# Attention: VectorE makes all low parts of the probabilities, where GpSimd made every second one

## The chip, the core and the metric

The kernel runs on one core of a Trainium2 chip. The metric is the device time of one execution in microseconds (us); lower is better. A core has five engines with a queue of instructions each, which run at the same time and wait for one another by semaphores: TensorE (PE in the rows; its weight loads are PEld), VectorE (DVE), ScalarE (ACT), GpSimd (POOL) and SyncE (SP), which here only issues DMAs. Every engine works off its own queue in order, so an instruction that waits holds up all that stands behind it.

## The reference

The program is a backbone of two layers over 1024 latent tokens with 1024 channels and a context of 256 tokens. The first layer has gated linear attention beside a latent attention (MLA), the second a Fourier mixing beside a spatial gate. The change touches only the latent attention:

```python
MLA_HEADS = 8
MLA_SCALE = (MLA_NOPE + MLA_ROPE) ** -0.5          # 64 + 32

def mla_attend(q_nope, q_rope, k_nope, k_rope, v):
    s = (jnp.einsum('bqhd,bkhd->bhqk', q_nope, k_nope, preferred_element_type=jnp.float32)
         + jnp.einsum('bqhr,bkr->bhqk', q_rope, k_rope, preferred_element_type=jnp.float32)) * MLA_SCALE
    p = jax.nn.softmax(s, axis=-1).astype(v.dtype)
    return jnp.einsum('bhqk,bkhd->bqhd', p, v)
...
    o_ml = mla_latent_blocks(qn_l, qr_l,
                             jnp.concatenate([kn_c, kn_l], 1),
                             jnp.concatenate([krot_c, krot_l], 1),
                             jnp.concatenate([vm_c, vm_l], 1))
    y_mla = o_ml * jax.nn.silu(mg_l)
```

There are 1024 queries and 1280 keys (latent tokens and context) for each of eight heads.

## The kernel before

All products are made with fp32r operands in two parts: a high part (the value rounded to fp32r, by ScalarE, line L136) and a low part (the value less its high part, a subtraction of two tiles, line L141). Three matmuls then stand for one: high by high, high by low, low by high (`mm3`, L146 to L148). `split` makes the two parts; its argument `lo_eng` says which engine makes the low part, VectorE if none is given.

The attention works head by head (0 to 7), in `mla`. For a head, `attend` goes over two halves of 512 queries and ten blocks of 128 keys, 20 steps. A step makes a block of scores in a PSUM bank, keys by queries (three matmuls, L1073 to L1075, tile `pss`), ScalarE takes their exponential into SBUF (L118, tile `pexp`), ScalarE makes the high part (L136) and one engine the low part (L141), both into a tile `ph`. Up to five steps later (`LAG`) `second` multiplies the values with them, into a bank `psav`: value high by probability high (L1057), value low by probability high (L1058), value high by probability low (L1059). Only L1059 needs the low part. At the end of a half ScalarE makes the reciprocal of the sums, and VectorE two products, L1066 (two SBUF inputs) and L1067 (one from PSUM).

The engine of a low part is chosen here, where `n` counts the steps of a head:

```python
            k.split(p, None, hi=ph[:, 0, :], lo=ph[:, 1, :], lo_eng=nc.gpsimd if LO_ENG[n % len(LO_ENG)] else None)
...
PREP, LAG, MAXT, EARLY = 1.4, 5, 1.1, 2
LO_ENG = (0, 1)
```

While a head runs, the next one is prepared (`mla_prep`): DMAs from SyncE's queue put its keys and queries in place (L181), then TensorE makes score blocks for the row maxima, for each of eight groups of 128 queries a trio of products over 512, 512 and 256 keys (L998, tile `psm`), and VectorE reduces each of them (L999, tile `mx`). VectorE then takes the maximum of the trios (L1002, tile `m`), TensorE transposes it (L1005), VectorE copies it (L1007) and a DMA from GpSimd's queue puts it into the queries as their 97th row. In heads 6 and 7 GpSimd also multiplies rows of the output weights with a gate (`out_weight`, L1140, tile `owr`), of which ScalarE and VectorE make high and low parts.

A weighted round robin (`weave`) merges these streams, and a scheduler then fixes each engine's order at build time. All score and value products share eight PSUM banks, and the SBUF tiles come from shared pools, so an engine that reads a tile late also gives its buffer back late.

Of the kernel before, what the change touches and what calls it, by code (L numbers as in the profile page):

```python
# [1011 lines left out]
def mla(k):  # L1012
# [28 lines left out]
    def attend(hd):  # L1041
# [27 lines left out]
        for n, (s, j) in enumerate(steps):  # L1069
# [8 lines left out]
            ph = k.b4(F32R, (P, 2, 512), name="ph")  # L1078
            k.split(p, None, hi=ph[:, 0, :], lo=ph[:, 1, :], lo_eng=nc.gpsimd if LO_ENG[n % len(LO_ENG)] else None)
            pp[s, j] = (ph[:, 0, :], ph[:, 1, :])  # L1080
# [29 lines left out]


PREP, LAG, MAXT, EARLY = 1.4, 5, 1.1, 2
LO_ENG = (0, 1)


def even_pre(k):
# [500 lines left out]
```

## Time and profile before

| | |
|---|---|
| median of 3 timed runs | 1145.99 us (1145.76 to 1149.88) |
| the profiled execution | 1150.75 us, span 1149.0 us |
| TensorE busy over the span | 1093.9 us, 95% |
| VectorE busy | 748.1 us, 65% |
| ScalarE busy | 562.2 us, 49% |
| GpSimd busy | 260.2 us, 23% |
| mean granted TensorE clock | 0.981 |

The span goes from the first instruction to the last; the execution's own time holds about 2 us more. Times in rows are counted from the span's start. "Idle before" in a row names what ended the engine's wait. Matmuls are pipelined: one of 512 columns shows some 0.40 us, and the next starts about 0.23 us after it. Several short instructions of one kind in a row stand as one row with their count (x5). The granted clock is 1.00 at TensorE's full 2.4 GHz.

### The profile page before, as it was taken

What the parts mean: (1) busy time and instruction counts of PE and PEld (TensorE: products, weight loads), DVE (VectorE), ACT (ScalarE), POOL (GpSimd) and SP (SyncE); (2) the same over time, 40 slices, a digit from 0 to 9 for tenths busy, and PEclk for the clock granted to TensorE, in tenths of its full rate; (3) what the DMA queues carried; (4) which work ended last, traced back from release to release, by engine and by line L of the source; (5) the groups of instructions that cost most, each with busy time, mean ns of one, the idle gap of its engine ahead of it and who ended that gap; (6) DMA issues with size and microseconds to landing.
All of it is one profiled execution on the core that took longest, in us unless ns stands there. A gap on an engine that the chain in (4) does not pass through costs nothing.

```text
span 1149.0 us, 14557 instructions
## 1 busy us (share of the span) xinstructions
PE 1093.9 (95%) x5288; PEld 867.0 (75%) x5288; DVE 748.1 (65%) x1264; ACT 562.2 (49%) x965; POOL 260.2 (23%) x260
## 2 busy tenths in 40 slices
PE   5889999899999999999999999999999999999997
PEld 3668778788677877767677666888788888888885
DVE  6867694866755685776777677798536633664544
ACT  6285655576563367857777768313422223332000
POOL 3520000000000023423324356443101000122111
PEclk8989999999999999999999999999999999999999
DMA  9635563333535752113302424323400311125111
GB/s 369 246 125 192 206 225 101 133 124 106 194 98 197 217 168 51 34 37 88 70 2 49 124 73 126 132 111 121 143 30 1 110 37 55 56 67 207 56 55 55
DMA packets 41753, 131.89 MB, mean 115 GB/s; under 512 B 5674, under 2 KB 7466, under 8 KB 41683
## 3 DMA queue, kind: packets, MB, share of 16 engines
q1 hardware_dynamic: 35578, 114.77, 31.0%
q0 software_dynamic: 3312, 10.26, 2.3%
q10 hardware_dynamic: 2792, 5.94, 1.3%
q8 instruction: 41, 0.67, 0.2%
q14 instruction: 30, 0.24, 0.1%
HBM read 98.37 MB, written 20.36 MB: 103 GB/s over the span
## 4 chain that ended last, share of the span: by engine, by line
PE 72%; DVE 11%; ACT 6%; issue 4%; POOL 3%; DMA 3%; SPq 0%; POOLq 0%; DVEq 0%; ACTq 0%
PE ps L146 11%; PE ps L148 10%; PE ps L147 10%; PE pso L146 4%; PE pso L148 4%; PE pso L147 4%; PE psm L998 3%; PE pss L1073 3%; PE pss L1074 2%; PE pss L1075 2%; PE psav L1059 2%; PE psav L1057 2%; PE psav L1058 2%; DVE acc L810 1%; DMA qh<-qrh 1%
## 5 line engine op out<-in xcount | busy, mean ns | idle before, releaser
L141 POOL TENSOR_TENSOR ph<-pexp,ph 128x512 fp32r<-128x512 f32 x80 | 108.0, 1354 | 171.5 <-ACT ph L136 143.3
L118 ACT ACTIVATE pexp<-pss 128x512 f32<-128x512 f32 x160 | 93.2, 595 | 64.6 <-PE pss L1075 63.0
L999 DVE TENSOR_REDUCE mx<-psm 128x1 f32<-128x512 f32 (+1 forms) x192 | 102.2, 592 | 13.4 <-PE psm L998 13.0
L146 PE MATMUL ps<-h,hi 128*128 128x512 f32 x256 | 104.0, 418 | 5.4 <-ACT h L331 2.3
L148 PE MATMUL ps<-h,lo 128*128 128x512 f32 x256 | 103.8, 406 | 3.6 <-DVE lo L308 1.7
L141 DVE TENSOR_TENSOR ph<-pexp,ph 128x512 fp32r<-128x512 f32 x80 | 76.2, 957 | 44.3 <-ACT ph L136 42.6
L147 PE MATMUL ps<-h,hi 128*128 128x512 f32 x256 | 102.7, 401 | 0.8 <-DVE h L332 0.8
L146 PE MATMUL pso<-hi,yh 128*128 128x512 f32 x256 | 99.8, 390 | 0.0
L147 PE MATMUL pso<-lo,yh 128*128 128x512 f32 x256 | 99.7, 390 | 0.0
L148 PE MATMUL pso<-hi,yl 128*128 128x512 f32 x256 | 99.0, 389 | 0.0
L136 ACT CAST ph<-pexp 128x512 fp32r<-128x512 f32 x160 | 95.2, 620 | 2.8
L141 DVE TENSOR_TENSOR lo<-wraw,hi 128x1024 fp32r<-128x1024 f32 x37 | 47.0, 1283 | 74.7 <-ACT hi L136 69.7
L146 PE MATMUL ps<-h1h,hi 128*128 128x512 f32 x192 | 75.1, 391 | 0.0
L148 PE MATMUL ps<-h1h,lo 128*128 128x512 f32 x192 | 74.7, 389 | 0.0
L147 PE MATMUL ps<-h1l,hi 128*128 128x512 f32 x192 | 74.7, 389 | 0.0
L1140 POOL TENSOR_TENSOR owr<-owr,rowB 128x1024 f32<-128x1024 f32 x16 | 43.6, 2733 | 118.4 <-DMA owr<-wo 118.4
L1059 PE MATMUL psav<-ph,V 128*96 128x512 f32 x160 | 64.0, 400 | 2.1 <-POOL ph L141 1.1
L1057 PE MATMUL psav<-ph,V 128*96 128x512 f32 x160 | 63.4, 396 | 0.2
L146 PEld LDWEIGHTS ps<-h,hi 128*128 128x128 f32 x256 | 49.0, 193 | 18.3 <-ACT h L331 3.8
L148 PEld LDWEIGHTS ps<-h,lo 128*128 128x128 f32 x256 | 49.2, 192 | 17.5 <-DVE lo L308 2.9
L147 PEld LDWEIGHTS ps<-h,hi 128*128 128x128 f32 x256 | 49.6, 194 | 10.9 <-DVE h L332 1.4
L148 PEld LDWEIGHTS pso<-hi,yl 128*128 128x128 f32 x256 | 48.1, 188 | 10.1
(364 smaller groups left out, 2612.6 us busy)
## 6 DMA issues: line engine op xcount, KB each, us to landing
aw<-ada SPq DMA_DIRECT2D x32, 512.0 KB, 7.5
araw<-ada SPq DMA_DIRECT2D x32, 512.0 KB, 4.8
wraw<-we SPq DMA_DIRECT2D x16, 512.0 KB, 7.5
owr<-wo SPq DMA_DIRECT2D x16, 512.0 KB, 3.5
xr<-x SPq DMA_DIRECT2D x16, 512.0 KB, 6.8
wraw<-wd SPq DMA_DIRECT2D x12, 512.0 KB, 3.5
xt<-x SPq DMA_DIRECT2D x8, 512.0 KB, 6.4
kt<-kn SPq DMA_DIRECT2D x16, 256.0 KB, 3.6
```

What stands on the lines that cost most here:

```text
L118: r = self.nc.scalar.activation(out=out, in_=in_, func=func, **kw)
L136: self.nc.scalar.copy(out=hi, in_=src)
L141: (lo_eng or self.nc.vector).tensor_tensor(out=lo, in0=src, in1=f32(hi), op=ALU.subtract)
L146: t.matmul(out, lhs[0], rhs[0], start=start, stop=False)
L147: t.matmul(out, lhs[0], rhs[1], start=False, stop=False)
L148: return t.matmul(out, lhs[1], rhs[0], start=False, stop=stop)
L998: T.matmul(ps[:, :n], q[0][0:96, i * P:(i + 1) * P], cols(kt[0], s, n)[0:96], start=True, stop=True)
L999: nc.vector.reduce_max(out=mx[:, i, b:b + 1], in_=ps[:, :n], axis=AX.X)
L1057: T.matmul(a[0:96, :], vhi(j, hd), hi, start=j == 0, stop=False)
L1059: T.matmul(a[0:96, :], vhi(j, hd), lo, start=False, stop=j == NK - 1)
L1073: T.matmul(ps, kc[0], q[0][:, o], start=True, stop=False)
L1140: k.nc.gpsimd.tensor_tensor(out=raw, in0=raw, in1=k.ogate, op=ALU.mult)
```

## The change

One tuple is cut to its first entry, so that `LO_ENG[n % len(LO_ENG)]` is 0 for every step and `lo_eng` is never GpSimd in the attention.

```diff
 PREP, LAG, MAXT, EARLY = 1.4, 5, 1.1, 2
-LO_ENG = (0, 1)
+LO_ENG = (0,)
```

The scheduler puts the instructions in another order from there on. On GpSimd's queue, over the whole attention, with `ph` the parts of the probabilities, `qh<-mr` the maxima's DMAs and `owr` the output weights, the difference begins so:

```order
 L1022 MEMSET V 128x8x32 x9
-L141 TENSOR_TENSOR ph<-pexp,ph 128x512 x6
+L181 DMA qh<-mr 1x8x128 x6
+L1140 TENSOR_TENSOR owr<-owr,rowB 128x1024 x2
 L181 DMA qh<-mr 1x8x128
-L141 TENSOR_TENSOR ph<-pexp,ph 128x512 x11
```

All 80 low parts leave the queue; the seven DMAs and the eight `owr` products remain.

On VectorE's queue in head 1, from the first maxima for head 2 to their end (`ph<-pexp,ph` is a low part, `mx<-psm` a maximum, `rl` and `mg` the end of a half), this stood before:

```order
L999 TENSOR_REDUCE mx<-psm 128x1 x2
L1066 TENSOR_TENSOR rl<-rl,mg 64x512
L999 TENSOR_REDUCE mx<-psm 128x1
L1067 TENSOR_TENSOR mg<-psav,rl 64x512
L999 TENSOR_REDUCE mx<-psm 128x1
L141 TENSOR_TENSOR ph<-pexp,ph 128x512
L999 TENSOR_REDUCE mx<-psm 128x1 x3
L141 TENSOR_TENSOR ph<-pexp,ph 128x512
L999 TENSOR_REDUCE mx<-psm 128x1 x6
L141 TENSOR_TENSOR ph<-pexp,ph 128x512
L999 TENSOR_REDUCE mx<-psm 128x1 x6
L141 TENSOR_TENSOR ph<-pexp,ph 128x512
```

and there stands now:

```order
L1067 TENSOR_TENSOR mg<-psav,rl 64x512
L141 TENSOR_TENSOR ph<-pexp,ph 128x512
L999 TENSOR_REDUCE mx<-psm 128x1 x3
L141 TENSOR_TENSOR ph<-pexp,ph 128x512
L999 TENSOR_REDUCE mx<-psm 128x1 x3
L141 TENSOR_TENSOR ph<-pexp,ph 128x512 x2
L999 TENSOR_REDUCE mx<-psm 128x1 x3
L141 TENSOR_TENSOR ph<-pexp,ph 128x512
L999 TENSOR_REDUCE mx<-psm 128x1 x3
L141 TENSOR_TENSOR ph<-pexp,ph 128x512
L999 TENSOR_REDUCE mx<-psm 128x1 x3
L141 TENSOR_TENSOR ph<-pexp,ph 128x512
```

Where six maxima followed each other, a low part now stands behind every trio.

On VectorE's queue in head 6, behind the first 13 maxima, with the low part of an output weight (`lo<-owr,hi`), this stood before:

```order
L141 TENSOR_TENSOR lo<-owr,hi 128x1024
L999 TENSOR_REDUCE mx<-psm 128x1
L141 TENSOR_TENSOR ph<-pexp,ph 128x512 x2
L999 TENSOR_REDUCE mx<-psm 128x1
L141 TENSOR_TENSOR ph<-pexp,ph 128x512
L999 TENSOR_REDUCE mx<-psm 128x1
L141 TENSOR_TENSOR ph<-pexp,ph 128x512
L999 TENSOR_REDUCE mx<-psm 128x1 x2
L141 TENSOR_TENSOR ph<-pexp,ph 128x512
L999 TENSOR_REDUCE mx<-psm 128x1 x6
```

and there stands now:

```order
L141 TENSOR_TENSOR lo<-owr,hi 128x1024
L141 TENSOR_TENSOR ph<-pexp,ph 128x512 x8
L999 TENSOR_REDUCE mx<-psm 128x1 x2
L141 TENSOR_TENSOR ph<-pexp,ph 128x512
L999 TENSOR_REDUCE mx<-psm 128x1 x3
L141 TENSOR_TENSOR ph<-pexp,ph 128x512
L999 TENSOR_REDUCE mx<-psm 128x1 x3
L141 TENSOR_TENSOR lo<-owr,hi 128x1024
L141 TENSOR_TENSOR ph<-pexp,ph 128x512
L999 TENSOR_REDUCE mx<-psm 128x1 x3
```

Twelve low parts and two of weights stand between the first maximum and the last in place of five and one.

## Rows read from the trace of the kernel before

**Rows 1.** Windows: the attention; span, busy us and count of each engine, clock, DMA.

```profile
416.00:718.00 302.00, 291.12 (x1241) 211.00 (x1240) 216.02 (x333) 224.39 (x398) 123.31 (x92) 0.99 0.25 64
```

**Rows 2.** Waits of TensorE in 416 to 718: total us, times, longest.

```profile
PE psm L998 <- DVE mx L999: 2.1, 2, 1.2
PE pss L1073 <- DVE mx L999: 2.0, 2, 1.3
PE psm L998 <- DMA ql<-qrl: 1.7, 1, 1.7
```

**Rows 3.** Groups by form, VectorE in 416 to 718: busy us, mean ns, idle before.

```profile
L141 DVE TENSOR_TENSOR ph<-pexp,ph 128x512 fp32r<-128x512 f32 x80 | 76.2, 957 | 44.3 <-ACT ph L136 42.6 <-issue 0.9 <-POOL ph L141 0.4
```

**Rows 4.** Timeline of VectorE in heads 1 and 2: start us, duration us, instruction, [idle before].

```profile
459.27 2.82 DVE L999 TENSOR_REDUCE mx<-psm 128x1 f32<-128x512 f32 x5
462.06 0.69 DVE L141 TENSOR_TENSOR ph<-pexp,ph 128x512 fp32r<-128x512 f32 x1
462.67 1.01 DVE L999 TENSOR_REDUCE mx<-psm 128x1 f32<-128x256 f32 x2
463.81 0.68 DVE L1066 TENSOR_TENSOR rl<-rl,mg 64x512 f32<-64x512 f32 x1
...
477.06 0.17 DVE L1002 TENSOR_REDUCE m<-mx 128x8 f32<-128x24 f32 x1
...
503.39 4.67 DVE L999 TENSOR_REDUCE mx<-psm 128x1 f32<-128x512 f32 x9
507.97 0.68 DVE L141 TENSOR_TENSOR ph<-pexp,ph 128x512 fp32r<-128x512 f32 x1
```

**Rows 5.** Timeline of TensorE: the transposes of the maxima in heads 0 to 3.

```profile
437.65 0.27 PE L1005 MATMUL psmt<-ident,m 128*8 128x128 f32 x1
...
478.43 0.27 PE L1005 MATMUL psmt<-ident,m 128*8 128x128 f32 x1
...
511.88 0.27 PE L1005 MATMUL psmt<-ident,m 128*8 128x128 f32 x1 [0.17 <-DVE m L1002]
...
560.13 0.27 PE L1005 MATMUL psmt<-ident,m 128*8 128x128 f32 x1
```

**Rows 6.** Timeline of VectorE: ends of the maxima stretches of heads 0, 2, 3, 6.

```profile
420.43 0.69 DVE L999 TENSOR_REDUCE mx<-psm 128x1 f32<-128x512 f32 x1
...
436.81 0.17 DVE L1002 TENSOR_REDUCE m<-mx 128x8 f32<-128x24 f32 x1
...
493.08 3.75 DVE L999 TENSOR_REDUCE mx<-psm 128x1 f32<-128x512 f32 x7 [0.91 <-PE psm L998]
...
511.66 0.17 DVE L1002 TENSOR_REDUCE m<-mx 128x8 f32<-128x24 f32 x1
...
542.44 2.21 DVE L999 TENSOR_REDUCE mx<-psm 128x1 f32<-128x512 f32 x4
...
559.90 0.17 DVE L1002 TENSOR_REDUCE m<-mx 128x8 f32<-128x24 f32 x1
...
645.66 3.93 DVE L999 TENSOR_REDUCE mx<-psm 128x1 f32<-128x512 f32 x7 [3.80 <-PE psm L998]
...
671.47 0.18 DVE L1002 TENSOR_REDUCE m<-mx 128x8 f32<-128x24 f32 x1
671.66 1.23 DVE L141 TENSOR_TENSOR lo<-owr,hi 128x1024 fp32r<-128x1024 f32 x1
```

**Rows 7.** Timeline of GpSimd and VectorE in heads 6 and 7: products of output weights.

```profile
649.47 2.38 POOL L1140 TENSOR_TENSOR owr<-owr,rowB 128x1024 f32<-128x1024 f32 x1 [8.16 <-DMA owr<-wo]
649.88 2.52 DVE L1066 TENSOR_TENSOR rl<-rl,mg 64x512 f32<-64x512 f32 x1 [0.28 <-ACT rl L118]
...
716.43 11.81 POOL L1140 TENSOR_TENSOR owr<-owr,rowB 128x1024 f32<-128x1024 f32 x4
```

**Rows 8.** Waits of TensorE's weight loads in 672 to 718.

```profile
PEld psav L1059 <- POOL ph L141: 4.7, 7, 1.1
```

**Rows 9.** Windows of 2 us in head 4: the granted clock is the last number but two.

```profile
574.00:576.00 2.00, 2.00 (x6) 1.51 (x6) 1.68 (x4) 1.16 (x3) 1.27 (x1) 0.50 0.00 0
```

## The prediction

> **What bounds the kernel now.** I read the windows first, because the change touches one stage only. In the attention (416 to 718 us) TensorE is busy 291 of 302 us [rows 1]; VectorE 216, GpSimd 123. So TensorE's own work sets the length of this stage, and 10.9 us is all that waits can still give back there, with a few us of low clock. Who ends TensorE's waits is in the chain of waits [rows 2]: the row maxima of VectorE, the DMAs that move the next head's queries, and, small, GpSimd's low parts. The groups by form [rows 3] show VectorE's 80 low parts with a mean of 957 ns, well above the 690 of one that is left alone [rows 4].
>
> VectorE is not the bound on average, but it is in places. In seven of the eight heads TensorE also makes the score blocks for the next head's maxima: eight trios `psm` (512, 512 and 256 columns), each followed on VectorE by three reductions L999. I call this the maxima stretch. It ends with L1002 on VectorE, and TensorE's transpose L1005 waits for that, in its queue, with the next products behind it. In head 1 (the second) VectorE works from 459.27 us and reaches L1002 at 477.06 [rows 4]; the transpose starts at 478.43 [rows 5], so VectorE has 1.15 us to spare (L1005 came 0.22 us behind L1002 in head 2, 511.66 to 511.88 [rows 5, 6]). In heads 2 and 3 it has nothing to spare [rows 5, 6].
>
> **The change, part by part.** Every second low part moves from GpSimd's queue to VectorE's, 80 instructions. Prices are those of an undisturbed VectorE [rows 4]: a low part takes 0.61 us of the queue (462.06 to 462.67), a normalizing product L1066 or L1067 is taken as much (its row reads 0.68 where the low part's reads 0.69), a trio of maxima 1.53 (nine instructions, 503.39 to 507.97, are three trios).
>
> Off VectorE goes what GpSimd cost it. 80 low parts at 957 ns in place of 690 are 21 us. On goes 80 x 0.61 = 48.8 us. The net is about +28 us on 216, that is 244 of 302 us: no overload on average, and outside the maxima stretches a low part per 1.4 us of TensorE work (six products at 291.12/1241 = 0.235 us [rows 1]) leaves room. So outside them the move costs nothing: what covers it is VectorE's idle time.
>
> Inside them it counts. By the order of instructions a stretch held 5, 5, 4, 5, 4, 5 and 5 low parts (heads 0 to 6) and now holds 7, 10, 7, 8, 7, 10 and 12. The stretch on VectorE is then: start, eight trios (12.24), low parts at 0.605, two normalizing products where they lie inside (1.21), and waits for ScalarE. Of those waits I know the present ones, as the rest of the stretch, and keep half, since a longer queue hides a part of them; none and all are the two bounds.
>
> Head 1: 12.24 + 5 x 0.605 + 1.21 = 16.48 of 17.79 us now, so 1.31 of waits. After: 459.27 + 12.24 + 6.05 + 1.21 + 0.65 = 479.42, transpose at 479.64 against 478.43: +1.2 us (bounds +0.6 and +1.9). Head 5 has the same order, +1.2.
> Head 2: 15.87 of 18.58 now (493.08 to 511.66 [rows 6]), 2.71 of waits. After: 493.08 + 12.24 + 4.24 + 1.21 + 1.35 = 512.12, transpose 512.34 against 511.88: +0.5 (0 to +1.8). Head 4 has the same seven low parts, but its stretch is long now for low clock (below): +0.1 (0 to +1.8).
> Head 0: three low parts stand ahead of the first maximum, where there was one, so it starts at 420.43 + 2 x 0.605 = 421.64. Then 12.24 + 7 x 0.605 = 438.1; with 0.5 of waits (half of the present 436.81 - 420.43 - 15.27 = 1.1) the transpose is at 438.8 against 437.65: +1.1 (+0.6 to +1.7).
> Head 3: 15.27 of 17.46 now [rows 6], 2.19 of waits. After: 542.44 + 12.24 + 4.84 + 1.1 = 560.62, transpose 560.84 against 560.13: +0.7 (0 to +1.8).
> Together +4.8 us (about +1.8 to +10.9).
>
> Head 6 is the one where GpSimd hurts now. There it also scales output weights (`owr`), and VectorE's operations with two SBUF inputs stand still meanwhile: L1066 takes 2.52 us at 649.88, while GpSimd's `owr` runs from 649.47 for 2.38 [rows 7]. VectorE needs 25.81 us for the stretch [rows 6], of which the undisturbed work is 12.24 + 5 x 0.605 + 1.21 + 1.23 (the low part of an `owr`, 671.66) = 17.7. After: 12.24 + 12 x 0.605 + 1.21 + 2.46 = 23.2. The collisions with low parts on GpSimd are gone, but two `owr` operations remain, and each can hold VectorE for 0 to 2.4 us; with the 1.84 seen in both places (2.52 less 0.68) it is 26.9: +1.0 (-2.6 to +2.2).
> Head 7 has no maxima. There TensorE waits 4.7 us at weight loads for GpSimd's low parts [rows 8], seven times; a load stands about one product, 0.235 us, ahead of its own, so about 4.7 - 7 x 0.235 = 3 reach the products. They go. But GpSimd, now idle, starts the last four `owr` as soon as they land and no longer at 716.43 [rows 7], in the midst of the last low parts; I take half of the gain back: -1.5 (-3 to +2).
> The moved POOL queue also sends the seven small DMAs `qh<-mr` earlier; no wait for one is seen now, so nothing is taken for it. TensorE has as many products as before between a head's last score block and the next maxima, so the waits for query DMAs [rows 2] stay.
>
> Clock: behind a wait for a query DMA (1.7 us [rows 2]) the granted clock fell to 0.50 in 574 to 576 [rows 9], from the 2.4 to the 1.2 GHz level: 1.0 us lost in that slice, taken as 1.5 with its flanks. One or two more such dips are possible with longer waits; the sum holds none.
>
> Sum: +4.8 + 1.0 - 1.5 = +4.3 us on a span of 1149.0 and an own time of 1150.75. That execution lies 4.8 us above the median of the three timed runs, 1145.99, to which I add the difference: 1150.3 us, +0.4%.
>
> The Trainium skill (Perfetto Trace Analysis, Optimizing Scalar/DVE Operations) says that offloading from a saturated VectorE even to GpSimd may make sense, and adds that the two share an SBUF read port, so that it might not help. The first half speaks against this change, and it is rival A below; the second half speaks for it, and rival B is what it would give.
>
> **Rivals.** About 0.5% (5.7 us) is what a measurement here can tell from no change.
> A, slower: VectorE becomes the bound of every maxima stretch. Place: L1002 and the banks that TensorE gets back from L999. The 28 more low parts inside the seven stretches cost 28 x 0.605 = 16.9 us, of which the present waits in VectorE's queue hide part; with all waits kept heads 0 to 5 give +10.9, with heads 6 and 7 as summed +10.4, with one clock dip +11.9: 1158. It decides from the point at which more than half of the waits remain. For it: heads 2 and 3 have no slack now. Against it: the waits are for ScalarE, and a queue that is late no longer waits.
> B, faster: the low parts never delay TensorE, and the collisions vanish. Then TensorE gets back about 3 in head 7 and most of the VectorE waits, 4.1 [rows 2], with one dip, 1.5: -8.6, 1137. For it: the 21 us of inflated low parts; against it: the counts above, and the `owr` collision, which starts the large wait of head 6, stays. The Trainium skill (SBUF — State Buffer, Who interferes with whom) has the mechanism: a VectorE operation with two SBUF inputs and a GpSimd one that reads SBUF exclude each other for a whole instruction; the 2.52 us row agrees.
> C, nothing: the delay at the transpose is made up, since VectorE and ScalarE catch up before TensorE runs dry, and head 7's gain pays for the rest: -1 to +1, 1146.
>
> **How the numbers follow.** Forecast (small loss, +1 to +5.7) 0.38; A (over +5.7) 0.36; C 0.15; B (over -5.7) 0.11. So faster 0.11, same 0.53, slower 0.36. The likeliest time is 1150.3 in its own range of 1147 to 1151.7. The range leaves out half of B and the far end of A: 1142.5 to 1158.
>
> **What would show it.** VectorE busy near 240 us in the attention, low parts at about 690 ns but for those beside `owr`; GpSimd at 15 to 26 us in place of 123. The transposes L1005 of heads 1 and 5 wait about 1 us or more for L1002; waits on GpSimd's low parts are gone in head 7; TensorE's idle time stands near 15 us in place of 10.9. It is wrong if those transposes start as early as now, if TensorE waits at L1059 for VectorE's low parts in the middle of heads, or if the clock dips are more than two.

## The result: 1.4% slower

The changed kernel takes 1162.76 us (median of four runs, 1160.52 to 1168.01) against 1145.88 us (four runs, 1144.81 to 1149.88) of the kernel before: ratio 1.014, 95% interval 1.0115 to 1.0165. That is 16.9 us, where +4.3 was forecast, and outside the range. The profiled execution took 1163.51 us with a span of 1161.7, so it is typical of its kernel; that of before lies 4.8 us above its median, which is why the two traces differ by only 12.7 us. Two executions in the runs below took far longer than all others, one of 1547 us with steps 3 to 14 shared and one of 2793 us of the kernel before; they stand in the medians and count in no ratio.

First the page, its line of busy time by engine and two of its costliest groups (busy us, mean ns of one, idle before and its releaser):

```profile
PE 1099.3 (95%) x5288; PEld 869.4 (75%) x5288; DVE 775.4 (67%) x1344; ACT 563.2 (48%) x965; POOL 151.4 (13%) x180
...
L141 DVE TENSOR_TENSOR ph<-pexp,ph 128x512 fp32r<-128x512 f32 x160 | 118.0, 756 | 33.5 <-ACT ph L136 32.9
...
L1059 PE MATMUL psav<-ph,V 128*96 128x512 f32 x160 | 64.7, 404 | 5.6 <-DVE ph L141 5.5
```

The window that answers to [rows 1], and, grouped by form in the same window, the low parts that answer to [rows 3]:

```profile
416.00:718.00 302.00, 287.03 (x1207) 206.90 (x1205) 238.60 (x402) 220.56 (x390) 16.44 (x13) 0.97 0.24 61
```

```profile
L141 DVE TENSOR_TENSOR ph<-pexp,ph 128x512 fp32r<-128x512 f32 x156 | 109.7, 721 | 33.5 <-ACT ph L136 32.9
```

VectorE's load is close to the forecast (238.6 us here, with 156 of the 160 low parts, against 244 in the sum), and a low part now takes 721 ns on average in this window where it took 957. But in the same 302 us TensorE got through 34 matmuls fewer (1207 against 1241), and the attention isn't over at 718. TensorE's longest waits, from the chain of waits over 414 to 730 us, are these (total us, times, longest):

```profile
PE psav L1059 <- DVE ph L141: 5.5, 5, 1.9
PE psmt L1005 <- DVE m L1002: 4.4, 3, 3.5
PE psm L998 <- DMA qh<-qnh: 2.1, 1, 2.1
```

For the third, a DMA of the next head's queries, there stood one of 1.7 us before [rows 2]; the first two stood nowhere near this size (0.6 and 0.3 us). To see in which heads the time went, I follow TensorE's transposes L1005, one for each of heads 0 to 6, from its first score product (L1073) to its last product with the values (L1059). First the kernel before (heads 0 to 3 are in [rows 5]), then the changed one, heads 0, 1, 2, 3, 5 and 6:

```profile
416.17 0.80 PE L1073 MATMUL pss<-qh,kt 97*128 97x512 f32 x1
...
631.39 0.28 PE L1005 MATMUL psmt<-ident,m 128*8 128x128 f32 x1
...
671.94 0.27 PE L1005 MATMUL psmt<-ident,m 128*8 128x128 f32 x1
...
717.11 0.40 PE L1059 MATMUL psav<-ph,V 128*96 128x512 f32 x1
```

```profile
414.60 0.80 PE L1073 MATMUL pss<-qh,kt 97*128 97x512 f32 x1
...
437.39 0.27 PE L1005 MATMUL psmt<-ident,m 128*8 128x128 f32 x1
...
478.13 0.27 PE L1005 MATMUL psmt<-ident,m 128*8 128x128 f32 x1 [0.46 <-DVE m L1002]
...
511.99 0.27 PE L1005 MATMUL psmt<-ident,m 128*8 128x128 f32 x1
...
561.52 0.27 PE L1005 MATMUL psmt<-ident,m 128*8 128x128 f32 x1
...
634.75 0.27 PE L1005 MATMUL psmt<-ident,m 128*8 128x128 f32 x1 [0.43 <-DVE m L1002]
...
678.35 0.37 PE L1005 MATMUL psmt<-ident,m 128*8 128x128 f32 x1 [3.54 <-DVE m L1002]
...
728.78 0.39 PE L1059 MATMUL psav<-ph,V 128*96 128x512 f32 x1
```

Counted from the first score product, the transpose of head 5 stands at 215.22 us before (631.39 - 416.17) and at 220.15 after (634.75 - 414.60): heads 0 to 5 lost 4.9 us. That of head 6 stands at 255.77 and 263.75, another 3.1. The last product ends at 301.34 (717.51) and 314.57 (729.17): the last piece, nearly all of it head 7, lost 5.3 more. So the attention is 13.2 us longer in the trace, and of this 8.3 us arise behind the transpose of head 5, where -0.5 was forecast.

What happens in head 7 stands in the timeline, GpSimd and VectorE first, then TensorE, 714 to 727 us:

```profile
714.87 2.50 POOL L1140 TENSOR_TENSOR owr<-owr,rowB 128x1024 f32<-128x1024 f32 x1 [27.61 <-DMA owr<-wo]
715.16 2.76 DVE L141 TENSOR_TENSOR ph<-pexp,ph 128x512 fp32r<-128x512 f32 x1
717.60 8.12 POOL L1140 TENSOR_TENSOR owr<-owr,rowB 128x1024 f32<-128x1024 f32 x3 [0.23 <-DMA owr<-wo]
717.95 0.69 DVE L1067 TENSOR_TENSOR mg<-psav,rl 64x512 f32<-64x512 f32 x1
718.66 7.61 DVE L141 TENSOR_TENSOR ph<-pexp,ph 128x512 fp32r<-128x512 f32 x3
```

```profile
717.97 0.48 PE L1059 MATMUL psav<-ph,V 128*96 128x512 f32 x1 [1.89 <-DVE ph L141]
...
720.77 0.48 PE L1059 MATMUL psav<-ph,V 128*96 128x512 f32 x1 [1.16 <-DVE ph L141]
...
723.54 0.47 PE L1059 MATMUL psav<-ph,V 128*96 128x512 f32 x1 [1.84 <-DVE ph L141]
```

One GpSimd product runs beside one VectorE low part, four times in a row: each low part then takes 2.1 to 2.9 us in place of 0.69, and TensorE, which needs one for every step, waits 1.2 to 1.9 us for each of three of them. L1067, which reads one of its two inputs from PSUM, took its usual 0.69 us beside the second product. In the kernel before these four products ran at 716.43 [rows 7], behind GpSimd's own last low part in its queue:

```profile
715.02 1.45 POOL L141 TENSOR_TENSOR ph<-pexp,ph 128x512 fp32r<-128x512 f32 x1 [1.75 <-ACT ph L136]
```

Now nothing stands ahead of them there, and they start as their loads land.

The last view is the granted clock. These are all stretches of the attention in which it fell below full, first of the changed kernel (the third in two parts), then of before (the clock is the last number but two):

```profile
573.50:577.50 4.00, 4.00 (x13) 3.19 (x12) 3.78 (x7) 1.46 (x3) 0.00 (x0) 0.57 0.00 0
659.00:666.50 7.50, 7.46 (x21) 5.15 (x20) 7.47 (x13) 7.34 (x14) 0.00 (x0) 0.54 0.02 3
676.00:678.30 2.30, 0.00 (x0) 0.00 (x0) 2.30 (x6) 2.25 (x5) 0.00 (x0) 0.57 0.00 0
678.30:683.50 5.20, 5.15 (x14) 3.67 (x15) 4.67 (x6) 2.95 (x6) 2.93 (x2) 0.53 0.18 54
724.00:728.00 4.00, 3.62 (x11) 2.25 (x10) 4.00 (x5) 0.00 (x0) 1.72 (x1) 0.57 0.00 0
```

```profile
573.00:577.00 4.00, 4.00 (x13) 3.23 (x12) 3.00 (x6) 2.90 (x5) 1.27 (x1) 0.57 0.00 0
655.00:659.00 4.00, 4.00 (x12) 2.98 (x13) 3.97 (x5) 4.00 (x8) 2.56 (x2) 0.57 0.02 4
```

A single dip has a mean clock of 0.57 over 4 us, 1.7 us lost (4 x 0.43); a double one 0.54 over 7.5, 3.4 us. Before has two single dips, 3.4 us. After has two single and two double ones, 10.2 us. The 6.8 us between them are half of the 13.2, but 1 us of them costs nothing, since TensorE was idle in 676 to 678.3 anyway. Of head 7's 5.3 us, 2.4 are the rest of the dip that began in head 6 (5.2 x 0.47), and 1.7 the dip at 724. The two new ones begin after TensorE has waited: 676 inside the 3.54 us at the transpose of head 6, 724 behind the three waits of head 7.

### The profile page after: what moved, and what is told of

Same layout as the page of the kernel before. It is cut to its first block, busy times and chain, and to the rows that moved or that the text cites. A ratio compares the mean times of both kernels' runs of the same rounds, so it can differ in the third digit from the quotient of the medians.

```text
span 1161.7 us, 14479 instructions
## 1 busy us (share of the span) xinstructions
PE 1099.3 (95%) x5288; PEld 869.4 (75%) x5288; DVE 775.4 (67%) x1344; ACT 563.2 (48%) x965; POOL 151.4 (13%) x180
## 4 chain that ended last, share of the span: by engine, by line
PE 67%; DVE 14%; ACT 9%; issue 4%; POOL 3%; DMA 2%; SPq 0%; POOLq 0%; DVEq 0%; ACTq 0%
PE ps L146 10%; PE ps L148 10%; PE ps L147 10%; PE pso L146 4%; PE pso L147 4%; PE pso L148 4%; DVE mx L999 3%; PE pss L1073 2%; PE psm L998 2%; PE psav L1059 2%; PE pss L1074 2%; PE pss L1075 2%; DVE ph L141 2%; PE psav L1057 2%; PE psav L1058 2%
## 5 line engine op out<-in xcount | busy, mean ns | idle before, releaser
L141 DVE TENSOR_TENSOR ph<-pexp,ph 128x512 fp32r<-128x512 f32 x160 | 118.0, 756 | 33.5 <-ACT ph L136 32.9
L1059 PE MATMUL psav<-ph,V 128*96 128x512 f32 x160 | 64.7, 404 | 5.6 <-DVE ph L141 5.5
L146 PEld LDWEIGHTS pso<-hi,yh 128*128 128x128 f32 x256 | 48.2, 188 | 9.9
```

What stands on the lines that cost most here:

```text
L141: (lo_eng or self.nc.vector).tensor_tensor(out=lo, in0=src, in1=f32(hi), op=ALU.subtract)
L146: t.matmul(out, lhs[0], rhs[0], start=start, stop=False)
L1059: T.matmul(a[0:96, :], vhi(j, hd), lo, start=False, stop=j == NK - 1)
```

## The experiments

Two theories stood after this reading. **Theory 1:** VectorE's longer queue in the maxima stretches costs heads 0 to 5 about 5 us; in heads 6 and 7 the loss comes from GpSimd's products of the output weights, which exclude VectorE's operations with two inputs. **Theory 2:** the longer queue on VectorE is the whole loss, everywhere. All runs are compared with the kernel before on the same chip (its median there: 1146.27 us for the low parts by heads and the products on VectorE, 1146.19 for the single low part and the two kernels without products in head 6, 1146.06 for the other four); each median is good to about 2 us.

**Low parts by heads.** Three kernels go back to GpSimd's every second low part in some heads only, by a condition in the line of the low parts (L1079 of the kernel before); the diff is that of the first, the others have `hd >= 6` and `hd < 6` in its place:

```diff
-lo_eng=nc.gpsimd if LO_ENG[n % len(LO_ENG)] else None)
+lo_eng=nc.gpsimd if hd == 7 and LO_ENG[n % len(LO_ENG)] else None)
```

Head 7 alone shared:

> Heads 0 to 6 with all low parts on VectorE, head 7 shared with GpSimd as before. Theory 1 (in head 7 GpSimd's last four owr products, now free to run among the last low parts, hold VectorE, and TensorE waits at L1059): the 5.5 us of waits at L1059 for VectorE's low parts fall under 1.5, and the time falls by 4 to 7 us against the changed kernel, to about 1157. Theory 2 (VectorE's longer queue in the maxima stretches is the whole loss; head 7 has no maxima): 1161 to 1164, as changed.

Measured 1155.51 us, ratio 1.0082 (1.0062 to 1.0102). The waits at L1059 for VectorE's low parts fall to 1.4 us, as theory 1 has it, and sharing head 7 as before gives back 7.3 us of the 16.9.

Heads 6 and 7 shared:

> Heads 0 to 5 with all low parts on VectorE, heads 6 and 7 shared as before. Theory 1: heads 0 to 5 cost what the prediction summed, about 5 us, so 1149 to 1153. Theory 2 (loss in proportion to the low parts added in maxima stretches, 21 of 28 in heads 0 to 5): 1146 + 17 x 0.75, about 1158.

Measured 1154.13, ratio 1.0063 (1.0038 to 1.0087). That is between the two: heads 0 to 5 alone cost 7.9 us by the medians, more than the 4.9 read from the trace.

Heads 0 to 5 shared:

> Heads 0 to 5 shared as before, heads 6 and 7 with all low parts on VectorE. Theory 1: the loss of heads 6 and 7, 8 to 12 us, so 1154 to 1158. Theory 2 (7 of 28 low parts): 1146 + 17 x 0.25, about 1150.

Measured 1155.27, ratio 1.007 (1.0048 to 1.0092). Heads 6 and 7 alone cost 9.0 us, as theory 1 has it, and the two halves add up: 7.9 + 9.0 = 16.9.

**The products on VectorE.** The changed kernel with the eight products of the first layer's output weights taken from GpSimd:

```diff
-    k.nc.gpsimd.tensor_tensor(out=raw, in0=raw, in1=k.ogate, op=ALU.mult)
+    (k.nc.vector if wsrc is k.A["wo0"] else k.nc.gpsimd).tensor_tensor(out=raw, in0=raw, in1=k.ogate, op=ALU.mult)
```

> The changed kernel with the first layer's owr products (L1140) on VectorE too, so that GpSimd reads nothing in the attention. VectorE gets eight more products of about 1.2 us, 9.8 us, in heads 6 and 7. Theory 1 (the two engines exclude each other): no VectorE operation in heads 6 and 7 is over 1.4 us, L1059 waits for low parts under 1.5 us, and the time is 1152 to 1158. Theory 2 (VectorE's load is the loss): slower than the changed kernel, 1165 or more.

Measured 1157.54, ratio 1.0096 (1.0074 to 1.0117). VectorE has eight operations more and the kernel is 5.2 us faster, so theory 2 falls for head 7: no VectorE operation of heads 6 and 7 takes more than 1.23 us, and the waits at L1059 for VectorE shrink from 5.5 us to 0.5. In head 6 the wait for L1002 stays (4.91 us), so it doesn't need a product on GpSimd.

**One low part that holds the products back.** If head 7 is lost because nothing stands ahead of the last four products on GpSimd, then a single low part in their way must bring it back:

```diff
-lo_eng=nc.gpsimd if LO_ENG[n % len(LO_ENG)] else None)
+lo_eng=nc.gpsimd if hd == 7 and n == 19 else None)
```

> The changed kernel, but GpSimd makes one low part of the 160: the last one of head 7. GpSimd takes its work in order, so the last four owr products stand behind it again, as they do in the kernel before, and can't start while VectorE makes the low parts ahead of it. Theory 1 (these four products are what costs the 7 us of head 7): nearly all of it comes back, 1155 to 1157.5 us, as with all ten of head 7's odd low parts on GpSimd (1155.5). Theory 2 (head 7 loses by the number of low parts that VectorE makes): one of ten is given back, under 1 us: 1161 to 1163 us.

Measured 1153.71, ratio 1.0063 (1.0042 to 1.0084): 9 us back for one low part of 160, more than theory 1 asked for and, within the noise, as much as for ten or for twenty. Its timeline on GpSimd, and TensorE at both ends of head 7:

```profile
716.92 1.39 POOL L141 TENSOR_TENSOR ph<-pexp,ph 128x512 fp32r<-128x512 f32 x1 [31.69 <-ACT ph L136]
718.28 11.81 POOL L1140 TENSOR_TENSOR owr<-owr,rowB 128x1024 f32<-128x1024 f32 x4
```

```profile
675.79 0.37 PE L1005 MATMUL psmt<-ident,m 128*8 128x128 f32 x1 [3.53 <-DVE m L1002]
...
718.37 0.47 PE L1059 MATMUL psav<-ph,V 128*96 128x512 f32 x1 [0.37 <-POOL ph L141]
```

GpSimd is idle for 31.69 us with the low part at the head of its queue; the four products run back to back as in [rows 7], and TensorE's last product with the values begins at 718.37. TensorE's waits at L1059 for VectorE are 0.2 us in all. This settles head 7: not how much VectorE has to do, but when GpSimd's products start.

**Heads 0 to 5.** Next, where in a head the longer queue hurts. All three kernels have heads 6 and 7 on VectorE alone and the products on VectorE, and differ in which steps of heads 0 to 5 are shared: all (`hd < 6` alone), 3 to 14 of 20 (the diff), or the others (`not 3 <= n < 15`):

```diff
-lo_eng=nc.gpsimd if LO_ENG[n % len(LO_ENG)] else None)
+lo_eng=nc.gpsimd if hd < 6 and 3 <= n < 15 and LO_ENG[n % len(LO_ENG)] else None)
```

All steps shared:

> Heads 0 to 5 as before (every second low part on GpSimd), heads 6 and 7 all on VectorE, and the owr products of the first layer on VectorE. Theory 1: the low parts of heads 6 and 7 cost nothing once GpSimd makes no long products beside them, so the time is that of the kernel before, 1145 to 1149 us. Theory 2: heads 6 and 7 cost what their longer queue costs, products or not; 1153 us or more, as measured with the products on GpSimd (1155.3).

Measured 1149.29, ratio 1.003 (1.001 to 1.005): 0.3 us above the range of theory 1, and clear of theory 2. It is 3.2 us above the kernel before, so these low parts and the products on VectorE together cost little, but not nothing.

Steps 3 to 14 shared:

> As the run before it, but in heads 0 to 5 GpSimd makes every second low part only in steps 3 to 14 of the 20, about where the maxima of the next head are taken; elsewhere VectorE makes all. Theory 1 (in heads 0 to 5 the loss is VectorE's queue in the maxima stretches): the same time as with all of heads 0 to 5 shared, within 2 us. Theory 2 (the loss of heads 0 to 5 is spread over all their steps, or is one of the clock): half of the 8 us comes back, 1151 to 1154 us.

Measured 1149.27, ratio 1.0024 (1.0004 to 1.0045).

The other steps shared:

> The complement: in heads 0 to 5 GpSimd makes every second low part only outside steps 3 to 14; in those VectorE makes all. Theory 1: the loss of heads 0 to 5 stays, 1155 to 1158 us (as with all on VectorE and the products on VectorE, 1157.5). Theory 2: half of it goes, 1151 to 1154 us.

Measured 1156.28, ratio 1.0092 (1.0061 to 1.0122). Sharing steps 3 to 14, six of a head's ten moved low parts, gives all; sharing the other four gives 1 us (of 1157.54, which has none), no more than the noise: the cost of heads 0 to 5 is VectorE's queue in the maxima stretches. Timeline of TensorE, first score product and transpose of head 5, with steps 3 to 14 shared, then with the others:

```profile
411.46 0.80 PE L1073 MATMUL pss<-qh,kt 97*128 97x512 f32 x1
...
625.75 0.28 PE L1005 MATMUL psmt<-ident,m 128*8 128x128 f32 x1
```

```profile
412.87 0.54 PE L1073 MATMUL pss<-qh,kt 97*128 97x512 f32 x1
...
632.83 0.27 PE L1005 MATMUL psmt<-ident,m 128*8 128x128 f32 x1 [0.47 <-DVE m L1002]
```

That is 214.29 against 219.96 us, 5.7 apart, of which 1.7 are a dip at 573 in head 4 that only the second trace has; head 6, the same in both, takes 2.4 us longer in the second, in which one dip more stands there:

```profile
658.00:662.00 4.00, 3.84 (x10) 2.67 (x11) 4.00 (x7) 4.00 (x9) 0.00 (x0) 0.57 0.00 0
```

That heads which are late draw a dip in the next is not shown: the longest wait of TensorE in the 13 us before this one is 0.5 us, and with no steps shared (1157.54 us) and with head 7 alone shared heads 0 to 5 are as late and no dip stands there. In the pair with all and no steps shared head 6 takes 1.7 us longer with equal dips, so the dip isn't all of it; the rest is open.

**Is there a better kernel?** Three tries. The kernel before with its products on VectorE (the second diff, on the kernel before):

> The kernel before (every second low part on GpSimd), with the eight products of the first layer's output weights on VectorE instead of GpSimd. Theory 1 (GpSimd's owr products and VectorE's two-input operations exclude each other in heads 6 and 7): the kernel before pays a little for it too (its 2.52 us product at 649.88, and GpSimd's low parts that come late in head 7), so this one is as fast or a little faster: 1143 to 1146 us. Theory 2 (what counts is the length of VectorE's own queue): eight more operations of some 1.2 us on VectorE in heads 6 and 7 make it slower, 1148 us or more.

Measured 1146.94, ratio 1.001 (0.9991 to 1.0029): neither. In the kernel before the last four products stood behind the low parts anyway, and the one collision in head 6 [rows 7] is not worth more than can be measured.

Then the products out of head 6, in two kernels: steps 3 to 14 of heads 0 to 5 shared, and the kernel before, both with the products on VectorE.

```diff
-PREP, LAG, MAXT, EARLY = 1.4, 5, 1.1, 2
+PREP, LAG, MAXT, EARLY = 1.4, 5, 1.1, 0
...
-        if hd == 6:
+        if hd == 6 and EARLY:
```

> GpSimd makes every second low part in steps 3 to 14 of heads 0 to 5 only, the owr products of the first layer are on VectorE (so far the run with the shared steps 3 to 14, 1149.3 us), and none of these products is taken in head 6 any more: the first two move into head 7. In head 6 TensorE then has no 4.9 us wait for the last reduction of the maxima (L1002), which now stands behind a product and its low part on VectorE, and the two stretches of low clock that follow it (3.4 us together) may go. Theory 1 (that wait is VectorE's queue): 4 to 8 us less, 1141 to 1145 us. Rival (the wait only moves into head 7, where the low parts then come late): no gain, 1148 to 1151 us.

> The kernel before (every second low part on GpSimd everywhere) with the owr products of the first layer on VectorE and none of them in head 6, as in the run before it. The wait for L1002 was 1.95 us here with two products in head 6 (1146.9 us). Theory 1: 2 to 4 us less, 1142 to 1145 us. Rival (moved, not removed): 1146 to 1149 us.

Measured 1148.1, ratio 1.0011 (0.9991 to 1.0032), and 1148.3, ratio 1.0015 (0.9998 to 1.0033): the rival was right. Timeline of the first of the two, TensorE in heads 6 and 7, and ScalarE in head 7, behind the transpose of head 6 in the kernel with steps 3 to 14 shared:

```profile
666.71 0.37 PE L1005 MATMUL psmt<-ident,m 128*8 128x128 f32 x1 [4.91 <-DVE m L1002]
```

```profile
665.95 0.27 PE L1005 MATMUL psmt<-ident,m 128*8 128x128 f32 x1 [0.84 <-DVE m L1002]
...
694.44 0.48 PE L1057 MATMUL psav<-ph,V 128*96 128x512 f32 x1 [1.99 <-ACT ph L136]
```

```profile
692.82 1.04 ACT L136 CAST hi<-owr 128x1024 fp32r<-128x1024 f32 x1 [0.47 <-DVE owr L1140]
693.77 1.66 ACT L136 CAST ph<-pexp 128x512 fp32r<-128x512 f32 x3
```

The wait at the transpose of head 6 falls from 4.91 to 0.84 us and its double dip goes; head 6 (from transpose to transpose) takes 35.1 us in place of 41.0. But head 7 takes 49.1 in place of 43.7: there the rounding of the weights (`hi<-owr`, ScalarE) waits for its product on VectorE with the probabilities' rounding behind it, TensorE waits 1.99 us for that, and a dip follows at 695. The wait was moved, and head 7 lost 5.4 us of the 5.9 that head 6 gained. No version here beats the kernel before.

## Why the prediction was wrong

**What bounds.** Right: TensorE bounds the stage on average, and VectorE bounds it in places. TensorE's idle time in 416 to 718 came to 15.0 us (302 - 287.03), as forecast; but the loss lies in the eleven us after 718 and in the clock, and neither shows in that number, since a TensorE at half clock counts as busy.

**Heads 0 to 5, +4.8.** Right in the trace, +4.9, and the place was right too, as the runs with steps 3 to 14 show. The prediction's counts hold for whole stretches, up to L1002 (ten low parts for five in head 1, twelve for five in head 6); of the lists of VectorE's queue under the change, those of head 1 begin behind its first maxima, and in that of head 6 eleven low parts, not twelve, stand before the last maximum. The split by heads was not right. Head 1's stretch on VectorE was sized well (457.85 to 477.91, 20.06 us, against 479.42 - 459.27 = 20.15), but its transpose came no later than head 0's delay had already made it (+1.3 in both); the two should not have been added, since VectorE began head 1's stretch hardly later than before (43.25 us behind the first score product, 43.10 before). Heads 3 and 4 lost more than was forecast (+1.3 and +1.0 against +0.7 and +0.1), which made up for it. The size was somewhat low: over all traces the transpose of head 5 stands 212.9 to 215.9 us behind the first score product where GpSimd shares the steps 3 to 14 (seven kernels) and 220.0 to 221.9 where it does not (six), 6 us apart on average, dips included. By the medians these heads cost 7 to 8 us; the last 1 to 2 us are not accounted for.

**Head 6, +1.0.** Its share was 3.1 us in the trace and 1.7 by difference of two medians (9.0 less the 7.3 of head 7), which is no more than their noise. More than half of the 3.1 is the clock. The kernel with head 7 alone shared has the same order on TensorE and VectorE in head 6 and no dip there; its window from transpose to transpose is this:

```profile
634.38:675.05 40.67, 34.80 (x146) 23.99 (x147) 32.23 (x53) 30.08 (x53) 5.66 (x3) 1.00 0.35 101
```

That is 40.67 us, where before took 40.55 with a single dip and after 43.60 with a double one ahead of the wait. The kernel with one low part on GpSimd, in the same order and with a single dip, took 41.4. With 1.7 us taken off for a single dip and 3.4 for a double one head 6 costs 0.9 to 1.8 us, so the +1.0 was near. The `owr` collision was there as expected (L1066 took 2.42 us beside a product from 653.81). Not foreseen was the 3.54 us at the transpose, and the dip that begins in it. In part that wait takes the place of others: TensorE's idle time in the head rose from 4.0 us only to 6.1. The wait stands with the products on VectorE as well and goes, but for 0.84 us, when they leave the head. These are the rows of VectorE ahead of that transpose:

```profile
672.77 1.23 DVE L141 TENSOR_TENSOR lo<-owr,hi 128x1024 fp32r<-128x1024 f32 x1 [0.74 <-ACT hi L136]
675.29 0.69 DVE L141 TENSOR_TENSOR ph<-pexp,ph 128x512 fp32r<-128x512 f32 x1 [1.29 <-ACT ph L136]
...
678.03 0.17 DVE L1002 TENSOR_REDUCE m<-mx 128x8 f32<-128x24 f32 x1
```

VectorE waits 2 us for ScalarE with the last maxima behind it in the queue. I had kept ScalarE's waits in the terms of heads 0 to 5 and left them out of head 6's.

**Head 7, -1.5: the step that failed.** The prediction says that GpSimd, now idle, starts the last four `owr` in the midst of the last low parts, and takes half of the gain back for it. The mechanism was right and the size was not: that half, 1.5 us, measured 7.3 to 9 us by the runs that give the products their old place, and head 7 as a whole came to +5.3 us in the trace. It should have been worked out, and the rows for it were there: [rows 7] has L1066 stretched to 2.52 us beside one product; four products in a row on four low parts are 4 x 1.84 = 7.4 us of VectorE, with no other work of TensorE to cover them, since in head 7 no maxima are left and each step needs its low part. The gain of 3 us on the other side was sized about right. With the products held back by one low part head 7 takes 43.0 us (675.79 to 718.84), with a dip of 1.6 us and four matmuls fewer (0.9 us) in it, against 45.6 before (671.94 to 717.51), with no dip: 2.5 us less as it stands, some 3 with both counted. TensorE's idle time for GpSimd's low parts, 1.1 us before, shows only part of this, since a product that starts up to 0.17 us late leaves no gap behind the one of 0.40 us ahead of it.

**Clock, none.** The second failed step. The sum held no dips, though one or two were called possible; the trace has 6.8 us more of them. A wait of TensorE was priced as its own length, but at the longest waits of this stage a dip begins: in all eight kernels that wait 3.5 to 5.0 us at the transpose of head 6 it does so inside the wait or up to 0.7 us behind it. At shorter waits it did in some kernels and not in others. The kernel before with its products on VectorE waits 1.95 us at that transpose, at 667.42, and its clock stays full:

```profile
667.00:671.00 4.00, 2.05 (x10) 1.29 (x9) 3.61 (x7) 3.98 (x7) 2.04 (x2) 1.00 0.00 0
```

No run here changes the clock alone, so how much of the loss it caused is read from the traces and not shown by an experiment.

**The rivals.** The time lies beyond A's 1158, on its side, but A's mechanism is only half of it: heads 0 to 5. B's first half came true (low parts of 721 ns in place of 957), and so did its 3 us in head 7 where the products are held back. In heads 0 to 5 the shorter low parts bought nothing that the runs show. The exclusion that B counted on worked the other way: the change took GpSimd's low parts away from VectorE's, and brought GpSimd's products on top of them. The Trainium skill (SBUF — State Buffer, Who interferes with whom) has it that a VectorE operation with two SBUF inputs and a GpSimd one that reads SBUF contend for a shared read port, one holding off the other; these rows agree (2.76 us beside a product of 2.50, and 0.69 for L1067 with its input from PSUM).

**What would show it.** Of the signs named for a wrong forecast two came: waits at L1059 for VectorE's low parts (at the end of head 7, not in the middle of heads), and more dips (two single and two double ones in place of two single ones). Of the signs named for a right one, the idle time near 15 us came, GpSimd's load (16.4 us), and the end of head 7's waits for GpSimd; the transposes of heads 1 and 5 waited for L1002, but 0.46 and 0.43 us where 1 or more was named.

## What to carry to other kernels

Work that is taken off an in-order queue also takes away what held back the instructions behind it. List what stands next in the emptied queue, when its inputs land, and what it then runs beside; here four products that had waited behind the last low part cost 9 us, more than half of the whole loss, and one operation left in place held them back. Price a long wait of TensorE with a clock dip behind it as well (1.7 or 3.4 us here), and a busy engine by its stretch: 12 of 20 steps held all of the loss of heads 0 to 5.

## What the runs showed of the hardware

The clock's loss comes in pieces: in the twelve kernels traced in this stage besides the one before, each dip took 1.7 us of TensorE's clock (mean 0.57 over some 4 us, between the 2.4 GHz level and the 1.2 GHz one) or 3.4 us when two follow each other; what of a dip falls into a wait costs nothing more. Their sum over the attention went from 1.7 us (the kernel before with its products on VectorE) to 10.2 (the changed kernel). That is about half of what differs between their attentions, 298.3 and 314.6 us; TensorE's idle time, 9.7 and 18.3 us, is the other half. The same instructions in the same order on TensorE and VectorE (head 6 of three kernels) drew a double, a single or no dip ahead of the wait at the transpose, and took 43.6, 41.4 and 40.7 us.

Beside a GpSimd product of 2.5 us VectorE's low part took 2.76 us, and three of them 7.61 beside three products in 8.12: the two engines took turns, one operation each, and a low part ended some 0.55 us behind the product beside it (717.92 and 717.37), so that VectorE's work ran at GpSimd's pace. L1067, with one input from PSUM, took 0.69 us beside such a product.
